# Attention scores from 64-row products of both heads of a pair, without doubled copies of q and k

## The chip, the cores and the metric

The kernel runs on one core of one Trainium2 chip. The core has a tensor engine (PE, with its weight loads listed apart as PEld), a vector engine (DVE), a scalar engine (ACT), GpSimd (POOL) and SyncE (SP, which issues the DMAs). The metric is the time of one execution in microseconds on the device; the kernel before took a median of 1409.52 us in 3 runs (1409.27 to 1410.91).

## The reference, cut to what matters

One layer of a hybrid decoder block on 1024 positions of width 1024, in float32. The attention has 8 heads of 64 and is strictly causal; its weights come from a running sum of log-sigmoids:

```python
def stick_breaking_attention(q, k, v):
    ...
        z = jnp.einsum("bhqd,bhkd->bhqk", qb, kb).astype(jnp.float32) * scale
        ...
        strict = s_idx < t_idx
        log_keep = jnp.where(strict, jax.nn.log_sigmoid(-z), 0.0)
        later = lax.cumsum(log_keep, axis=3, reverse=True) - log_keep
        w = jnp.where(strict, jnp.exp(jax.nn.log_sigmoid(z) + later), 0.0)
        outs.append(jnp.einsum("bhqk,bhkd->bhqd", w, vb.astype(jnp.float32)))

...
        h = rms_norm(x, norm_mix_pre[l])
        proj = h @ w_in[l]
        q, k, v, cb, cc, cx, g_att, g_conv = jnp.split(proj, IN_SPLITS, axis=-1)
        ...
        y_att = o.transpose(0, 2, 1, 3).reshape(b, s, ATT_WIDTH) @ w_att_branch[l]
        y_conv = (cb * causal_dwconv(cc * cx, conv_mix_w[l])) @ w_conv_branch[l]
        merged = jax.nn.sigmoid(g_att) * y_att + jax.nn.sigmoid(g_conv) * y_conv
        x = x + rms_norm(merged @ w_out[l], norm_mix_post[l])
        ...
        u = causal_dwconv(h @ w_up[l], conv_ffn_w[l])
        a, g = jnp.split(u, 2, axis=-1)
        f = (jax.nn.gelu(g, approximate=True) * a) @ w_down[l]
```

## The kernel before, in words

Every float32 matrix product is made from float16 halves: a number is split into a high half (a rounded copy, made by ACT) and a low half (the remainder, made by DVE), and a product takes three passes, high by high, high by low and low by high (`PASSES`). All matmuls use 128 rows of the array, with a weight load (LDWEIGHTS) ahead of each.

The program has these stages: normalising and transposing x, and v of the first four row tiles (to about 50 us); q and k of the first pair of heads (to 75); attention over four pairs `j` of heads (75 to about 420), with other projections mixed in as filling; the two branch products (`pywc`, `pywa`), the gates, the output projection, and then the feed-forward part to the end.

`qk_tile(j, which)` makes q or k of one pair: the 128 rows of its PSUM tile are two heads of 64, in two halves of 512 positions. For q it writes both halves of the split into `qtmp` and then copies each head twice with DVE (L369), so that `XA` and `XB` hold one head each on rows 0 to 63 and again on 64 to 127. For k (L374, L375) each head is a tile `K[:, h]` whose one 64 rows are the high half and the other 64 the low half. One 128-row product of `K` with the doubled high half of q is then both k-high by q-high and k-low by q-high, and a second with the doubled low half adds the other two: two matmuls for a head, four for a pair.

`attention(j)` runs over 12 units in a pair, 48 in all. A unit is one block of 128 keys against up to 512 queries, for both heads (units on the diagonal are 128, 256, 384 or 512 columns wide). `stage1` makes the scores z in PSUM, brings them to SBUF as `zc` (DVE), and takes exp, log and a split of the result, `sp` and `sh` (ACT, ACT, ACT, DVE). `stage2` sums with a triangular matrix into PSUM `A`, adds it to zc (DVE), and makes the split weights `w` (ACT, ACT, DVE); `stage2b` adds the rest of the block to A; `stage3` multiplies by v into PSUM `o`. PSUM holds one z, one A and one o of two banks each, and two banks `pm` for the filling. All these matmuls are recorded at the line of the helper `mm` (L453 before; L439 after the change, since lines move).

`merge` interleaves this with a generator of filling: v of the last four row tiles (in pair 0), q and k of the next pair, and the convolution's projections `pcc`, `pcx` and `pcb`; in pair 3 also `p_split` and the branch products `pywc`. After the last `pcb` matmul the convolution's result `pf` is multiplied (L408), its square summed (`jk_p`, L56), a scale is made through a one-column matmul `pr` (L74 and the small DVE lines behind it), and `p_split` splits it into `p` (L86, L87), which is what `pywc` (L436) reads.

The order on each engine is fixed when the program is built: a scheduler places instructions by priority and by its own estimate of when their inputs are there. Within an engine the order is then strict. `tc.high_priority()` around the attention stages puts them ahead of filling that is ready at the same time. The weights of the projections arrive by DMAs from SP (512 KB each) into a ring of tiles; q, k and most other large tiles come from a ring of 16 slots of 4 KB a row (`slab`).

Of the kernel before, what the change touches and what calls it, by code (L numbers as in the profile page):

```python
# [16 lines left out]
F16 = mybir.dt.float16  # L17
# [3 lines left out]
AF = mybir.ActivationFunctionType  # L21
ALU = mybir.AluOpType
AX = mybir.AxisListType

P = 128
T = 1024
# [8 lines left out]
PASSES = ((0, 0), (0, 1), (1, 0))  # L35


class Layer:
# [230 lines left out]
    def mixer(self, mid):  # L269
        tc, nc, a = self.tc, self.nc, self.a  # L270
        hT = self.hp.tile([P, 2, KD, T], F16, tag="hT", name="hT")
        with ExitStack() as ph1:
# [75 lines left out]
            stk = {}  # L348

            def qk_tile(j, which):  # L350
                w, inv = self.prep(f"{which}{j}")
                if which == "q":
                    stk[j] = dict(A=self.slot([P, 2, T], F16, f"XA{j}"), B=self.slot([P, 2, T], F16, f"XB{j}"),
                                  iq=inv)
                    tmp = self.slot([P, 2, T], F16, f"qtmp{j}")
                else:
                    stk[j]["K"] = self.slot([P, 2, T], F16, f"K{j}")
                s = stk[j]
                for c in range(2):
                    ps = pm.tile([P, NH], F32, tag="pm", name=f"p{which}{j}_{c}")  # L360
                    yield from self.cm_half(w[0], hT, ps, c)
                    sl = ds(c * NH, NH)
                    if which == "q":
                        nc.scalar.activation(tmp[:, 0, sl], ps, AF.Copy, scale=2.0 ** -15)
                        nc.vector.scalar_tensor_tensor(tmp[:, 1, sl], ps, 2.0 ** -15, tmp[:, 0, sl],
                                                       ALU.mult, ALU.subtract)
                        for h0, b in ((0, "A"), (64, "B")):
                            for d0 in (0, 64):
                                nc.vector.tensor_copy(s[b][d0:d0 + 64, :, sl], tmp[h0:h0 + 64, :, sl])  # L369
                    else:  # L370
                        for h0, b in ((0, "A"), (64, "B")):
                            K = s["K"][:, h0 // 64, :]
                            d0 = 64 - h0
                            nc.scalar.activation(K[h0:h0 + 64, sl], ps[h0:h0 + 64], AF.Copy, scale=2.0 ** -15)  # L374
                            nc.vector.scalar_tensor_tensor(K[d0:d0 + 64, sl], ps[h0:h0 + 64], 2.0 ** -15,  # L375
                                                           K[h0:h0 + 64, sl], ALU.mult, ALU.subtract)
                if which == "k":
                    cz = self.small(f"cz{j}", keep=True)
                    self.mul(cz[:, 0:1], s["iq"], inv)
                    self.mul(cz[:, 1:2], cz[:, 0:1], cst[:, 0:1])  # L380
                    s["cz"] = cz[:, 1:2]
                yield
# [61 lines left out]
            def attention(j):  # L444

                s = stk[j]
# [5 lines left out]
                def mm(out, w, mv, **kw):  # L452
                    nc.tensor.matmul(out, w, mv, skip_group_check=True, **kw)  # L453

                def stage1(u):
                    off, i, c, nm = u["off"], u["i"], u["c"], u["nm"]
                    tsl = ds(c * NH + off, NH - off)
                    z = pat.tile([P, 2, NH], F32, tag="z", name=f"z{nm}")
                    for h, b in enumerate("AB"):
                        mm(z[:, h, off:], s["K"][:, h, ds(i * P, P)], s[b][:, 0, tsl], start=True, stop=False)  # L460
                        mm(z[:, h, off:], s["K"][:, h, ds(i * P, P)], s[b][:, 1, tsl], start=False, stop=True)
                    zc = att.tile([P, 2, NH], F32, tag="zc", name=f"zc{nm}", bufs=3)

                    if u["diag"]:
                        nc.vector.scalar_tensor_tensor(zc[:, :, off:], z[:, :, off:], s["cz"],  # L465
                                                       self.clamp[:, :, :NH - off], ALU.mult, ALU.min)
                    else:
                        nc.vector.tensor_scalar(zc[:, :, off:], z[:, :, off:], s["cz"], 44.0,
                                                ALU.mult, ALU.min)

                    sp = att.tile([P, 2, NH], F32, tag="sp", name=f"sp{nm}", bufs=2)
                    nc.scalar.activation(sp[:, :, off:], zc[:, :, off:], AF.Exp)  # L472
                    nc.scalar.activation(sp[:, :, off:], sp[:, :, off:], AF.Ln, bias=self.one)
                    sh = att.tile([P, 2, 2, NH], F16, tag="sh", name=f"sh{nm}", bufs=2)
                    nc.scalar.activation(sh[:, 0, :, off:], sp[:, :, off:], AF.Copy)  # L475
                    nc.vector.tensor_tensor(sh[:, 1, :, off:], sp[:, :, off:], sh[:, 0, :, off:], ALU.subtract)  # L476
                    u["zc"], u["sh"] = zc, sh
# [47 lines left out]
                n = len(units)  # L525
                for k in range(n + 2):
                    if k < n:
                        with tc.high_priority():
                            stage1(units[k])
                        yield 6  # L530
                    if 0 <= k - 1 < n:
                        with tc.high_priority():
                            stage2(units[k - 1])
                        yield 8
                        with tc.high_priority():
                            stage2b(units[k - 1])
                    if 0 <= k - 2 < n:
                        with tc.high_priority():
                            stage3(units[k - 2])
                        yield 6  # L540
# [16 lines left out]
            for which in "qk":  # L557
                for _ in qk_tile(0, which):
                    pass
            for j in range(4):  # L560
                gens = []
                nf = 3 * 16 + 1
                if j == 0:
                    gens += [v_tile(tt) for tt in range(4, 8)]
                    nf += 32
                if j < 3:
                    gens += [qk_tile(j + 1, "q"), qk_tile(j + 1, "k")]
                    nf += 34
                gens.append(conv_tile(j))
                if j == 3:  # L570
                    gens += [p_split()] + [branch(0, d, pm) for d in range(8)]
                    nf += 65
                merge(attention(j), 240, chain(*gens), nf)
# [403 lines left out]
class Pair:  # L977
# [3 lines left out]
    A = {1: (0, 0), 2: (0, 1), 3: (3, 0), 4: (1, 1), 5: (2, 0), 6: (2, 1), 7: (1, 0)}  # L981
# [153 lines left out]
```

## Time and profile before

| what | value |
|---|---|
| median of 3 runs | 1409.52 us (1409.27 to 1410.91) |
| profiled execution, its time | 1407.68 us |
| its span, first to last instruction | 1405.9 us |
| PE busy | 1344.2 us (96%), 6447 matmuls |
| DVE busy | 1083.9 us (77%) |
| ACT busy | 856.6 us (61%) |
| DMA | 99.72 MB, 71 GB/s on average |
| granted PE clock, mean | 0.990 |

An engine is busy while one of its instructions runs; matmuls overlap each other by design, so a busy PE says that matmuls follow each other, and the time from one start to the next says at what rate. Idle time is put down to what released the engine. A row of a group reads: line, engine, operation, output<-inputs, shape, count, busy time in all, mean ns of one, idle time just before them and who ended it.

### The profile page before, as it was taken

To read this page: it belongs to the slowest core of one execution; us is meant where nothing else is said; L and a number is where in the kernel's file an instruction comes from. 1 tells how busy PE (TensorE), PEld (TensorE's weight loads), DVE (VectorE), ACT (ScalarE), POOL (GpSimd) and SP (SyncE) were. 2 spreads that over 40 slices of the span, in tenths; PEclk is the share of its full clock that TensorE was granted. 3 is DMA by queue.
4 is the path that set the end of the run, shared out by engine and by line. 5 is a ranking of instruction groups with operands and counts; after the bars stand their busy time and mean duration, and the time that the engine had idled before them with its cause. 6 is when DMAs were issued, how large, how long until landed. Compare 5 with 4: busy or idle time off the path is not lost. (4 is left out here: it accounts for less than half of the span.)

```text
span 1405.9 us, 16721 instructions
## 1 busy us (share of the span) xinstructions
PE 1344.2 (96%) x6447; PEld 626.9 (45%) x6447; DVE 1083.9 (77%) x1692; ACT 856.6 (61%) x1187; POOL 29.3 (2%) x47
## 2 busy tenths in 40 slices
PE   5999999999989999999998999999999999999997
PEld 3444454545434444444443444444444444444443
DVE  5758787887784797878777894994895796699747
ACT  6568788787873465776556467761761672476422
POOL 2000000000000000000111000000000000000001
PEclk9999999999999999999999999999999999999999
DMA  7111001010001102251331112121220311213115
GB/s 256 46 46 31 31 31 45 31 31 30 31 31 45 31 31 61 90 180 45 106 120 60 60 60 91 60 90 48 89 78 27 121 60 60 108 54 110 60 60 195
DMA packets 28369, 99.72 MB, mean 71 GB/s; under 512 B 3185, under 2 KB 3185, under 8 KB 28289
## 3 DMA queue, kind: packets, MB, share of 16 engines
q1 hardware_dynamic: 27792, 97.01, 20.4%
q0 software_dynamic: 496, 1.65, 0.4%
q8 instruction: 50, 0.82, 0.2%
q14 instruction: 31, 0.25, 0.1%
HBM read 90.25 MB, written 8.39 MB: 70 GB/s over the span
## 5 line engine op out<-in xcount | busy, mean ns | idle before, releaser
L1005 PEld LDWEIGHTS <-wh_u 128*128 128x128 f16 x1848 | 179.2, 98 | 222.7 <-issue 10.2
L904 PE MATMUL pd<-wdh,f 128*128 128x512 f16 x1056 | 234.1, 383 | 9.3 <-DVE wdh L87 5.1
L904 PEld LDWEIGHTS <-f 128*128 128x128 f16 x1056 | 104.1, 99 | 137.5 <-issue 13.3
L86 ACT ACTIVATE wh_u<-ws_u,sc 128x1024 f16<-128x1024 f32 (+1 forms) x66 | 64.2, 999 | 100.7 <-DVE sc L78 83.3
L910 DVE SCALAR_TENSOR_TENSOR yacc<-pd,sd,yacc 128x512 f32<-128x512 f32 x80 | 58.4, 746 | 69.6 <-PE pd L904 62.1
L1005 PEld LDWEIGHTS <-wh_g 128*128 128x128 f16 x588 | 56.8, 98 | 70.6 <-ACT wh_g L86 2.3
L719 PE MATMUL py<-wh_wo,m 128*128 128x512 f16 x384 | 84.7, 381 | 0.0
L87 DVE SCALAR_TENSOR_TENSOR wh_u<-ws_u,sc,wh_u 128x1024 f16<-128x1024 f32 (+1 forms) x66 | 71.8, 1099 | 7.1 <-ACT wh_u L86 7.1
L453 PE MATMUL A<-sh,tri 128*128 128x512 f16 (+3 forms) x352 | 71.5, 323 | 2.9 <-DVE zc L488 1.6
L493 DVE SCALAR_TENSOR_TENSOR w<-zc,w 128x1024 f16<-128x1024 f32 (+3 forms) x48 | 45.8, 955 | 25.0 <-ACT w L492 24.8
L1082 DVE SCALAR_TENSOR_TENSOR ugu<-cgu,cw_g,ugu 128x1023 f32<-128x1023 f32 (+1 forms) x44 | 56.2, 1278 | 10.9 <-ACT ugu L1080 10.5
L472 ACT ACTIVATE sp<-zc 128x1024 f32<-128x1024 f32 (+3 forms) x48 | 40.1, 836 | 29.9 <-DVE zc L465 20.4
L719 PEld LDWEIGHTS <-m 128*128 128x128 f16 x384 | 37.8, 99 | 44.7 <-issue 1.0
L1082 DVE SCALAR_TENSOR_TENSOR ua<-cau,cw_a,ua 128x1023 f32<-128x1023 f32 (+1 forms) x44 | 56.1, 1276 | 1.1 <-ACT ua L1080 1.0
L488 DVE SCALAR_TENSOR_TENSOR zc<-A,zc 128x1024 f32<-128x1024 f32 (+3 forms) x48 | 45.6, 950 | 8.3 <-PE A L453 8.1
L453 PE MATMUL o<-w,v 128*128 128x512 f16 (+3 forms) x192 | 46.0, 329 | 4.4 <-DVE w L493 3.1
L476 DVE TENSOR_TENSOR sh<-sp,sh 128x1024 f16<-128x1024 f32 (+3 forms) x48 | 45.6, 951 | 4.1 <-ACT sh L475 3.8
L309 PE MATMUL pv<-wh_v,hT 128*128 128x512 f16 x192 | 45.7, 389 | 2.5 <-ACT wh_v L86 1.7
L1080 ACT ACTIVATE ua<-cau,cw_a 128x1024 f32<-128x1024 f32 x22 | 25.1, 1139 | 37.1 <-DVE cau L1032 33.8
L56 ACT ACTIVATE jk_u<-ws_u 128x1024 bf16<-128x1024 f32 x44 | 46.3, 1053 | 0.8
L203 PE MATMUL pcx<-hT,wh_cx 128*128 128x512 f16 x192 | 46.3, 379 | 0.2 <-ACT u L404 0.2
L453 PEld LDWEIGHTS <-tri 128*128 128x128 f16 x352 | 32.4, 98 | 30.4 <-issue 3.7
(613 smaller groups left out, 2729.0 us busy)
## 6 DMA issues: line engine op xcount, KB each, us to landing
ws_u<-w_up_nt SPq DMA_DIRECT2D x44, 512.0 KB, 3.5
ds<-w_down SPq DMA_DIRECT2D x22, 512.0 KB, 6.0
wd<-w_down SPq DMA_DIRECT2D x22, 512.0 KB, 3.6
ws_g<-w_in_nt SPq DMA_DIRECT2D x14, 512.0 KB, 3.5
x<-x SPq DMA_DIRECT2D x8, 512.0 KB, 8.8
ws_wo<-w_out SPq DMA_DIRECT2D x8, 512.0 KB, 7.2
xr<-x SPq DMA_DIRECT2D x8, 512.0 KB, 4.1
x2d<-x SPq DMA_DIRECT2D x8, 512.0 KB, 2.9
```

Source lines behind the costliest of these rows:

```text
L56: self.nc.scalar.activation(self.junk(f"jk_{name}"), src, AF.Square, accum_out=acc)
L86: self.nc.scalar.activation(dst[:, 0, :], src, AF.Copy, scale=s)
L87: self.nc.vector.scalar_tensor_tensor(dst[:, 1, :], src, s, dst[:, 0, :], ALU.mult, ALU.subtract)
L203: nc.tensor.matmul(ps, w[:, wi, ds(k * P, P)], hT[:, hi, k, ds(c * NH, NH)], start=n == 0, stop=n == last)
L309: nc.tensor.matmul(pv, hT[:, hi, k, ds(tt * P, P)], wv[k // 2][:, wi, ds((k % 2) * NH, NH)], start=n == 0, stop=n == 3 * KD - 1)
L453: nc.tensor.matmul(out, w, mv, skip_group_check=True, **kw)
L493: nc.vector.scalar_tensor_tensor(w[:, 1, :, off:], zc[:, :, off:], 2.0 ** 14, w[:, 0, :, off:], ALU.mult, ALU.subtract)
L719: nc.tensor.matmul(ps[nh], m16[k][:, hi, ds(tt * P, P)], wo[k][:, wi, ds(nh * NH, NH)], start=k == 0 and p == 0, stop=k == 7 and p == 2)
L904: nc.tensor.matmul(ps, f16[g][k][:, hi, ds(tt * P, P)], w[k][:, wi, sl], start=n == 0, stop=n == 3 * GROUPS[g] - 1)
L910: nc.vector.scalar_tensor_tensor(y[:, sl], ps, sm[:, 0:1], y[:, sl], ALU.mult, ALU.add)
L1005: nc.tensor.matmul(ps, w[wt][:, wi, ds(wc * NH + k * P, P)], self.block(i, hi, k), start=first and n == 0, stop=n == 3 * KH - 1, skip_grou ...
L1082: nc.vector.scalar_tensor_tensor(u[:, lag:], c[:, :T - lag], sm[:, 2 - lag:3 - lag], u[:, lag:], ALU.mult, ALU.add)
```

## The change

q and k of a pair are now kept as they leave the projection: one tile each with the high and the low half, rows 0 to 63 for one head and 64 to 127 for the other. `qtmp`, `XA`, `XB` and the two-headed `K` are gone, and with them the copies; q and k are each converted by one ACT and one DVE instruction of 128 rows for each half of the positions.

The scores of a unit are made in three passes, as everywhere else in the kernel; the low by low product that the doubled tiles gave is left out. In each pass one matmul takes rows 0 to 63 of the array for the first head and one takes rows 64 to 127 for the second, each with its own bank of z. A unit has six matmuls of 64 rows where it had four of 128. A very high priority around each of them puts them ahead of everything else that is ready.

```diff
--- before.py
+++ after.py
@@ -350,30 +350,16 @@
             def qk_tile(j, which):
                 w, inv = self.prep(f"{which}{j}")
                 if which == "q":
-                    stk[j] = dict(A=self.slot([P, 2, T], F16, f"XA{j}"), B=self.slot([P, 2, T], F16, f"XB{j}"),
-                                  iq=inv)
-                    tmp = self.slot([P, 2, T], F16, f"qtmp{j}")
-                else:
-                    stk[j]["K"] = self.slot([P, 2, T], F16, f"K{j}")
+                    stk[j] = dict(iq=inv)
+                stk[j][which] = self.slot([P, 2, T], F16, f"{which}{j}")
                 s = stk[j]
                 for c in range(2):
                     ps = pm.tile([P, NH], F32, tag="pm", name=f"p{which}{j}_{c}")
                     yield from self.cm_half(w[0], hT, ps, c)
                     sl = ds(c * NH, NH)
-                    if which == "q":
-                        nc.scalar.activation(tmp[:, 0, sl], ps, AF.Copy, scale=2.0 ** -15)
-                        nc.vector.scalar_tensor_tensor(tmp[:, 1, sl], ps, 2.0 ** -15, tmp[:, 0, sl],
-                                                       ALU.mult, ALU.subtract)
-                        for h0, b in ((0, "A"), (64, "B")):
-                            for d0 in (0, 64):
-                                nc.vector.tensor_copy(s[b][d0:d0 + 64, :, sl], tmp[h0:h0 + 64, :, sl])
-                    else:
-                        for h0, b in ((0, "A"), (64, "B")):
-                            K = s["K"][:, h0 // 64, :]
-                            d0 = 64 - h0
-                            nc.scalar.activation(K[h0:h0 + 64, sl], ps[h0:h0 + 64], AF.Copy, scale=2.0 ** -15)
-                            nc.vector.scalar_tensor_tensor(K[d0:d0 + 64, sl], ps[h0:h0 + 64], 2.0 ** -15,
-                                                           K[h0:h0 + 64, sl], ALU.mult, ALU.subtract)
+                    nc.scalar.activation(s[which][:, 0, sl], ps, AF.Copy, scale=2.0 ** -15)
+                    nc.vector.scalar_tensor_tensor(s[which][:, 1, sl], ps, 2.0 ** -15, s[which][:, 0, sl],
+                                                   ALU.mult, ALU.subtract)
                 if which == "k":
                     cz = self.small(f"cz{j}", keep=True)
                     self.mul(cz[:, 0:1], s["iq"], inv)
@@ -456,9 +442,12 @@
                     off, i, c, nm = u["off"], u["i"], u["c"], u["nm"]
                     tsl = ds(c * NH + off, NH - off)
                     z = pat.tile([P, 2, NH], F32, tag="z", name=f"z{nm}")
-                    for h, b in enumerate("AB"):
-                        mm(z[:, h, off:], s["K"][:, h, ds(i * P, P)], s[b][:, 0, tsl], start=True, stop=False)
-                        mm(z[:, h, off:], s["K"][:, h, ds(i * P, P)], s[b][:, 1, tsl], start=False, stop=True)
+                    for n, (hk, hq) in enumerate(PASSES):
+                        for h in range(2):
+                            d = ds(64 * h, 64)
+                            with tc.high_priority(10 ** 6):
+                                mm(z[:, h, off:], s["k"][d, hk, ds(i * P, P)], s["q"][d, hq, tsl],
+                                   start=n == 0, stop=n == 2)
                     zc = att.tile([P, 2, NH], F32, tag="zc", name=f"zc{nm}", bufs=3)
 
                     if u["diag"]:
```

Three places in the order show the effect. Names end in a buffer number; `z0_01` is the unit of pair 0 with key block 1, `A`, `sh`, `tri`, `o` and `v16` belong to attention's later stages, `pv`, `pcb` and `pywc` are filling. On PE, the scores of unit z0_01 before:

```order
L309 MATMUL pv5_738<-wh_v_3_182,hT_101 128x512
L453 LDWEIGHTS K0_611
L453 MATMUL z0_01_746<-XA0_497,K0_611 128x384
...
L453 LDWEIGHTS tri_98
L453 MATMUL A0_03_716<-sh0_03_684,tri_98 128x128
...
L453 MATMUL z0_01_746<-XB0_498,K0_611 128x384
```

The same unit in the changed program:

```order
L309 MATMUL pv5_728<-wh_v_2_179,hT_101 128x512
L439 LDWEIGHTS k0_601
L439 MATMUL z0_01_736<-q0_497,k0_601 128x384
...
L309 LDWEIGHTS hT_101
L309 MATMUL pv5_728<-wh_v_2_179,hT_101 128x512
```

The load and the matmul of z stand there six times in a row, with nothing between; before, matmuls of A stood among the four. That holds for all 48 units: before, 12 of them had other work inside, now none has.

On PE at the end of attention (pair 3, last key block 0), before:

```order
L436 MATMUL pywc0_1_3485<-p16_3_3432,wh_wc0_0_2891 128x512
L453 LDWEIGHTS v16_0_113
L453 MATMUL o3_17_3479<-w3_10_3885,v16_0_113 128x512
L436 LDWEIGHTS wh_wc0_0_2891
L436 MATMUL pywc0_0_3462<-p16_3_3432,wh_wc0_0_2891 128x512
```

And in the changed program:

```order
L203 MATMUL pcb3_1_3386<-hT_101,wh_cb3_0_2772 128x512
L439 LDWEIGHTS v16_0_113
L439 MATMUL o3_17_3509<-w3_10_3925,v16_0_113 128x512
...
L74 LDWEIGHTS ones_85
L74 MATMUL pr26_3448<-rb26_3445,ones_85 128x1
L74 LDWEIGHTS ones_85
L74 MATMUL pr27_3477<-rb27_3475,ones_85 128x1
L422 LDWEIGHTS wh_wc0_0_2905
L422 MATMUL pywc0_0_3492<-p16_0_3453,wh_wc0_0_2905 128x512
```

The last `o` matmuls of attention stood among the first `pywc`; now they stand right behind the last `pcb`, and between them and the first `pywc` there are only the two one-column matmuls `pr`.

On ACT at the same place, before:

```order
L492 ACTIVATE w3_12_3759<-zc3_12_3653 128x1024
L56 ACTIVATE jk_p3_3412,sm_p_449<-pf3_3301 128x1024
L56 ACTIVATE jk_wa2_0_3458,sm_wa2_3455<-ws_wa2_0_3456 128x1024
L472 ACTIVATE sp3_10_3805<-zc3_10_3803 128x1024
L473 ACTIVATE sp3_10_3805<-sp3_10_3805,one_89 128x1024
L490 ACTIVATE zc3_11_3734<-zc3_11_3734 128x1024
L475 ACTIVATE sh3_10_3808<-sp3_10_3805 128x1024
L492 ACTIVATE w3_11_3823<-zc3_11_3734 128x1024
L86 ACTIVATE p16_0_3423<-pf0_1440,sc25_3414 128x1024
```

In the changed program:

```order
L481 ACTIVATE w3_10_3925<-zc3_10_3843 128x1024
L507 ACTIVATE of3_10_3964<-o3_17_3509 64x512
L56 ACTIVATE jk_p3_3442,sm_p_449<-pf3_3327 128x1024
L507 ACTIVATE of3_10_3964<-o3_17_3509 64x512
L56 ACTIVATE jk_wa2_0_3488,sm_wa2_3485<-ws_wa2_0_3486 128x1024
L511 ACTIVATE o16_3_3036<-of3_10_3964 128x512
L86 ACTIVATE p16_0_3453<-pf0_1436,sc25_3444 128x1024
```

The square of pf (`jk_p3`) stood ahead of the last unit of attention on ACT and now stands behind it.

## The prediction

> **What bounds the kernel now.** I read the whole page first, then the busy time by stage, then what the tensor engine waits for inside the attention stage, then the order in time of its matmuls. The page first:
>
> ```profile
> span 1405.9 us, 16721 instructions
> PE 1344.2 (96%) x6447; PEld 626.9 (45%) x6447; DVE 1083.9 (77%) x1692; ACT 856.6 (61%) x1187; POOL 29.3 (2%) x47
> ```
>
> PE is busy nearly all the time, but a share over the span does not say whether it is the limit where the change is made. The scores are made between 75 and 400 us. The table by stage gives busy time with the number of instructions in brackets; the last three columns are granted PE clock, DMA share and GB/s:
>
> ```profile
> 75.00:400.00 325.00, 320.42 (x1685) 157.94 (x1683) 259.22 (x385) 261.35 (x351) 0.00 (x0) 1.00 0.10 31
> 400.00:420.00 20.00, 15.52 (x63) 6.35 (x62) 18.23 (x32) 16.55 (x20) 0.00 (x0) 0.91 0.08 27
> 420.00:480.00 60.00, 56.64 (x265) 25.53 (x264) 30.00 (x56) 23.20 (x38) 0.00 (x0) 1.00 0.15 45
> ```
>
> In the first row PE lacks 4.6 us of 325, while DVE and ACT are idle for 66 and 64. So in this stage a microsecond of PE work added or taken moves everything behind it, and a microsecond of DVE or ACT work does so only where PE waits for it. The second row is the end of attention, the one place where PE is short of work. All that PE waits for in the first row:
>
> ```profile
> PE A L453 <- DVE zc L488: 1.2, 2, 0.9
> PE z L453 <- DVE K L375: 0.9, 1, 0.9
> PE o L453 <- DVE w L493: 0.9, 1, 0.9
> PE o L453 <- ACT w L492: 0.7, 1, 0.7
> PE z L453 <- DVE zc L465: 0.6, 2, 0.4
> ```
>
> Eight short waits. Only one, 0.9 us for K, comes from the operands that the change makes differently.
>
> How much PE time a matmul takes is read from runs of equal matmuls in order of time (start, length, count):
>
> ```profile
> 149.52 0.28 PE L453 MATMUL z<-XA,K 128*128 128x128 f16 x2
> 150.18 1.89 PE L453 MATMUL A<-sh,tri 128*128 128x512 f16 x8
> 151.91 1.46 PE L203 MATMUL pcc<-hT,wh_cc 128*128 128x512 f16 x6
> 154.09 0.38 PE L453 MATMUL z<-XA,K 128*128 128x256 f16 x2
> 291.76 0.81 PE L453 MATMUL A<-sh,tri 128*128 128x384 f16 x4
> ```
>
> Eight of 512 columns begin at 150.18 and the next group at 151.91: 0.216 us from start to start. One record is 0.379 long (the group lasts 1.89 = 7 x 0.216 + 0.38). So a matmul needs 0.216 of the array and its result is there 0.379 after its start; the missing 0.163 lies beside the next matmul. The other widths give (0.81 - 0.326) / 3 = 0.162 for 384 columns, 0.38 - 0.272 = 0.109 for 256 and 0.28 - 0.219 = 0.06 for 128 (I use 0.056), with record lengths from 219 ns up:
>
> ```profile
> L453 PE MATMUL z<-XA,K x96: 219/351/379, 74.9 to 399.8; 128*128 128x512 f16 x48, 128*128 128x128 f16 x16, 128*128 128x256 f16 x16, 128*128 128x384 f16 x16
> L453 PE MATMUL z<-XB,K x96: 219/352/379, 76.0 to 400.2; 128*128 128x512 f16 x48, 128*128 128x128 f16 x16, 128*128 128x256 f16 x16, 128*128 128x384 f16 x16
> ```
>
> **The change part by part.** *Score matmuls.* Now 192 are issued: 96 x 0.216 + 32 x (0.162 + 0.109 + 0.056) = 31.2 us, four to a unit. The change issues six to a unit, 288. If the two of a pass share the array, a unit costs three spacings instead of four: 23.4 us, so -7.8. If they follow each other it costs six: 46.8, so +15.6. No row shows a 64-row product. The nearest is the weight load:
>
> ```profile
> L453 PEld LDWEIGHTS <-tri 128*128 128x128 f16 x352 | 32.4, 98 | 30.4 <-issue 3.7
> ```
>
> 98 ns of load for every matmul disappear inside the 0.216 spacing, so the array does take a second instruction while one streams, and the two of a pass touch different rows and different PSUM banks. I take -7.8. The Trainium skill (TensorE: Matmul & The Clock Gate, section Measured speedup vs the span model) reports row-packed matmuls as running side by side; no trace here shows it yet.
>
> *Going between 128 and 64 rows.* Each of the 48 units now goes into the 64-row shape and out of it: 96 turns, where before every matmul had one shape. The new order keeps the six together, so there are no more than 96. A turn costs nothing if the pipeline takes it like any other weight load, and at least the hidden 0.163 if the array must run empty first: 0 to 15.6 us, and with an exposed 98 ns load behind it 25.1. Nearest row: the trace has no other change of shape to go by, and the longest pipeline time that it does show is the 0.163; I take that, +15.6, and keep 0 and 25.1 for the range. The Trainium skill (TensorEngine Tiling (Array Packing), section Key Properties) says that a change of tiling mode drains the TensorE, without a price; by that rule the full 0.163 falls due and the sum stays as it is, without it the sum would be about -8.
>
> *Copies of q and k.* Mean ns stand before the last bar's idle time:
>
> ```profile
> L375 DVE SCALAR_TENSOR_TENSOR K<-pk,K 64x512 f16<-64x512 f32 x16 | 11.0, 689 | 4.0 <-ACT K L374 3.6
> L374 ACT ACTIVATE K<-pk 64x512 f16<-64x512 f32 x16 | 9.4, 590 | 1.3 <-PE pk L203 0.7 <-DVE K L375 0.4
> L369 DVE COPY XB<-qtmp 64x1024 f16<-64x1024 f16 x16 | 6.8, 423 | 0.2
> L369 DVE COPY XA<-qtmp 64x1024 f16<-64x1024 f16 x16 | 6.7, 417 | 0.2
> ```
>
> Gone are 32 copies (13.5 us) and 8 of the 16 K remainders (5.5) on DVE, and 8 activations (4.7) on ACT; one on 128 rows replaces two on 64, and I keep the duration. This lies beside PE work in the first stage, so nearly all of it is worth nothing. What it does give is the K wait at the first scores, -0.9. No DMA, POOL or SP instruction comes or goes.
>
> *The end of attention.* Freed DVE time lets the scheduler run attention further ahead of the projections that fill PE. Before, the last scores stood after the last projection pcb, and the last `A` and `o` mixed with waits: in the second stage row 61 full matmuls x 0.216 = 13.2 of 20 us, so 6.8 lost (part of it to the clock of 0.91). In the new order 48 pcb matmuls cover those steps, and these 6.8 go. But the last pcb also begins another chain: pf, its sum of squares, the scale, the split of p, and only then pywc. It used to run while attention finished. Now three `o` matmuls stand behind the last pcb, then PE stops. Durations of that chain, from before:
>
> ```profile
> 399.16 0.75 DVE L408 SCALAR_TENSOR_TENSOR pf<-pcb,cv,pf 128x512 f32<-128x512 f32 x1 [1.15 <-PE pcb L203]
> 401.07 1.04 ACT L56 ACTIVATE jk_p<-pf 128x1024 bf16<-128x1024 f32 x1
> 402.02 0.19 ACT L56 ACTIVATION_READ_ACCUMULATOR jk_p<-pf 128x1 f32 x1
> 402.24 1.06 ACT L56 ACTIVATE jk_wa<-ws_wa 128x1024 bf16<-128x1024 f32 x1
> 403.72 0.15 DVE L68 TENSOR_REDUCE sc<-sm_p 128x1 f32<-128x4 f32 x1
> 404.92 0.14 DVE L69 CAST rb<-sc 128x1 bf16<-128x1 f32 x1
> 405.91 0.19 PE L74 MATMUL pr<-rb,ones 128*128 128x1 bf16 x2
> 408.26 4.25 ACT L86 ACTIVATE p<-pf,sc 128x1024 f16<-128x1024 f32 x4
> 409.71 1.28 DVE L87 SCALAR_TENSOR_TENSOR p<-pf,sc,p 128x1024 f16<-128x1024 f32 x1
> 418.94 0.59 ACT L518 ACTIVATE of<-o 64x512 f32<-64x512 f32 x1 [3.36 <-PE o L453]
> 421.94 0.63 ACT L522 ACTIVATE o<-of 128x512 f16<-128x512 f32 x1 [0.76 <-DVE of L519]
> ```
>
> By ACT's new order, counted from the end of the last pcb (t = 0): the `o` matmuls free PE at 0.5 and end at 0.65; ACT does of until 1.3, then the square of pf and its read until 2.5; reduce and cast on DVE, so pr starts at 2.8: PE waited 2.3. ACT goes on with of (3.1), jk_wa (4.3), o16 (4.9) and p (6.0): pywc starts near 6.0, another 2.9. Its third pass needs the remainder on DVE, 1.28 later, about 1 more, and the next tile's somewhat less. Together 6.6. With nothing queued ahead on ACT the least is 3.6, and with a half-clock stretch as at 400 us 8.5. Taken 7.5, against 6.8 before: +0.7 (-3.2 to +1.7).
>
> *Sum.* -7.8 + 15.6 - 0.9 + 0.7 = +7.6 us on the profiled execution, which took 1407.7 us (1.8 around its span of 1405.9). It lies 1.8 below the 1409.5 median of the runs; I add the difference to that median: 1417.1, said as 1417. The remaining waits of the first stage are left at 3.7: PE gets slower there, so they could shrink to nothing or, with six scores now in one piece, grow a little.
>
> **The rivals.**
> 1. *The turn is cheap, so the kernel gets faster.* Place: the first 128-row matmul behind each six. For it: no row shows a drain, and dtype changes (the bf16 pr between f16 matmuls) cost none. Against: all pipelining in the trace is between matmuls of one shape. Without the 15.6 the sum is -8.0, 1401.5 us; it is zero at 8.0 / 96 = 83 ns a turn. The gain may not all arrive, since the shorter PE work meets the chain of DVE and ACT earlier; doubling the 3.7 us of waits would give 1405.
> 2. *The two of a pass follow each other.* +15.6 in place of -7.8: 1424.9 if turns are free, 1440.5 with them. For it: line 453's matmuls never overlap beyond 0.163. Against: the disjoint rows and banks.
> 3. *Weight loads no longer hide.* Passes two and three of a unit would each show one or two loads of 98 ns: 48 x 2 x 0.098 = 9.4, or 18.8, so 1426.5 to 1435.9. Against: the 98 ns are hidden everywhere now. The Trainium skill (TensorE: Matmul & The Clock Gate, section The mechanism) lets a load overlap a running matmul only when the row groups differ; this trace, where loads to the same 128 rows hide, already disagrees, which is why I give it little.
> 4. *The relief of DVE decides and PE does not.* Against: the 4.6 us of waits in 325. At most those go as well, 1413 with my turn price; it is inside my range.
>
> **How the numbers follow.** A change under 0.2% (2.8 us) can hardly be told from none. Per turn price: above 112 ns the sum is over +2.8, below 54 ns under -2.8. Chances: forecast, pairs share the array and a turn costs 112 to 260 ns (1412 to 1427), 0.55; the same with 54 to 112 ns, no change, 0.14; rival 1 below 54 ns, 0.13; rival 2, 0.10; rival 3, 0.08. Slower 0.55 + 0.10 + 0.08 = 0.73, same 0.14, faster 0.13. The range 1408 to 1431 leaves out rival 1 and the upper halves of rivals 2 and 3, about 0.2.
>
> **What would show it.** Pairs: the two z records of a pass start within some ns and a unit of 512 columns takes 3 x 0.216. Turns: from the last z to the next matmul, and from the matmul before to the first z, 0.379 or more instead of 0.216. Relief: no copies, and the first scores without the 0.9 wait. End: pr waits some 2.3 and pywc some 2.9 us after attention, near 415 to 425. I am wrong if these turns show 0.216 to 0.27, if six z take 1.3 us, or if waits for DVE grow well beyond 4.6 us between 75 and 400.

## The result, and the profile after

The changed kernel takes 1413.17 us (median of 7 runs, 1410.43 to 1414.92) against 1409.27 for the kernel before on the same chip (7 runs, 1406.69 to 1410.91). The ratio is 1.0031, 95% interval 1.0017 to 1.0044: slower by some 4.4 us by this ratio and by 3.9 by the two medians, where +7.6 was forecast. The profiled execution has a span of 1410.9 us, 5.0 more than before.

The first two lines of the page, after:

```profile
span 1410.9 us, 16871 instructions
PE 1345.0 (95%) x6543; PEld 616.1 (44%) x6543; DVE 1065.5 (76%) x1652; ACT 852.0 (60%) x1179; POOL 29.9 (2%) x47
```

There are 96 matmuls more and 40 DVE instructions less, as the change says; DVE works 18.4 us less, and the time is longer all the same. Where it goes shows in busy time by stage. From 73 to 400, 400 to 430 and 430 to 480 us, first before, then after:

```profile
73.00:400.00 327.00, 322.42 (x1694) 158.85 (x1693) 259.66 (x387) 262.83 (x353) 0.00 (x0) 1.00 0.10 32
400.00:430.00 30.00, 24.68 (x106) 10.54 (x105) 23.72 (x43) 21.56 (x28) 0.00 (x0) 0.94 0.07 21
430.00:480.00 50.00, 47.48 (x223) 21.34 (x221) 24.51 (x44) 18.18 (x29) 0.00 (x0) 1.00 0.17 52
```

```profile
73.00:400.00 327.00, 320.58 (x1771) 147.05 (x1768) 247.40 (x356) 263.61 (x350) 0.00 (x0) 1.00 0.10 30
400.00:430.00 30.00, 23.60 (x98) 9.92 (x97) 18.47 (x38) 12.20 (x17) 0.00 (x0) 0.89 0.11 35
430.00:480.00 50.00, 47.48 (x223) 21.54 (x222) 22.21 (x43) 18.04 (x29) 0.00 (x0) 1.00 0.14 43
```

The third row is alike in both. In the first PE idles 6.4 us instead of 4.6; in the second, where attention ends, it idles 6.4 instead of 5.3 at a clock of 0.89 instead of 0.94.

How the scores stand on the array shows one unit of 512 columns in order of time, on PE and then on its weight loads, in the kernel after:

```profile
109.76 1.03 PE L203 MATMUL pq<-hT,wh_q 128*128 128x512 f16 x4
110.72 0.82 PE L439 MATMUL z<-q,k 64*128 64x512 f16 x6
111.48 0.60 PE L203 MATMUL pq<-hT,wh_q 128*128 128x512 f16 x2
```

```profile
109.98 0.31 PEld L203 LDWEIGHTS <-wh_q 128*128 128x128 f16 x2
110.72 0.33 PEld L439 LDWEIGHTS <-k 64*128 64x128 f16 x6 [0.42 <-DVE zc L477]
111.47 0.33 PEld L203 LDWEIGHTS <-wh_q 128*128 128x128 f16 x3 [0.42 <-issue]
```

Six matmuls last 0.82 us: two spacings of 0.22 and one record of 0.376. The raw starts behind this row are 110.722, 110.726, 110.949, 110.952, 111.165 and 111.168, so the two of a pass begin 3 or 4 ns apart and share the array. On both sides there is a step: the last `pq` began at 110.41 and the first score at 110.72, 0.31 instead of 0.216, and from the last score to the next `pq` it is again 0.31. Every undisturbed turn of this run costs 0.095 to 0.096, counted from the start of a pass, after 128 columns as after 512; after a one-column matmul it is 0.07. The loads tell how: among equal shapes the next load starts 2 ns after the running matmul, but across a turn none starts until 0.307 after the last matmul began, that is 0.09 after its columns have passed and 0.07 before its record ends; the matmul then follows the load by 4 ns. So at a turn nothing new enters for 0.09 us, and the stop of 0.096 is shorter than the 0.163 that waiting for the last result would take; the ends of matmul records are modelled, so how empty the array then is the trace does not show. The Trainium skill (TensorEngine Tiling (Array Packing), section Key Properties) says that a change of tiling mode drains the TensorE. This trace agrees in that the stream stops at every turn; the price here is 96 ns.

Adding up the starts of all matmuls between the first score and the first gate (`pgc`), with 0.216, 0.162, 0.109 and 0.056 for a matmul and for each turn what it measured, 0.07 to 0.096:

| from the first score to the first gate, us | before | after |
|---|---|---|
| score matmuls | 31.2 | 24.0 |
| all other matmuls | 357.0 | 357.4 |
| turns | 0 | 8.8 (95) |
| the rest: waits and half clock | 16.8 | 21.1 |
| sum | 404.9 | 411.3 |

The 0.4 more of other matmuls are two of `pk` that now stand behind the first scores. The first score starts 2.0 us earlier after the change (1.7 of it is a stretch at half clock near 50 us that only the profile of before has), and the later stages differ by 0.6.

The end of attention, on which the prediction's last term rested, after:

```profile
408.37 0.81 PE L439 MATMUL o<-w,v 128*128 128x512 f16 x3
408.57 0.75 DVE L394 SCALAR_TENSOR_TENSOR pf<-pcb,cv,pf 128x512 f32<-128x512 f32 x1 [3.71 <-PE pcb L203]
409.71 1.04 ACT L56 ACTIVATE jk_p<-pf 128x1024 bf16<-128x1024 f32 x1
411.28 0.22 PE L74 MATMUL pr<-rb,ones 128*128 128x1 bf16 x2 [2.11 <-DVE rb L71]
413.06 4.25 ACT L86 ACTIVATE p<-pf,sc 128x1024 f16<-128x1024 f32 x4
414.24 1.01 PE L422 MATMUL pywc<-p,wh_wc 128*128 128x512 f16 x2 [2.74 <-ACT p L86]
415.56 4.81 PE L422 MATMUL pywc<-p,wh_wc 128*128 128x512 f16 x11 [0.31 <-DVE p L87]
```

The three `o` matmuls, 2.1 us of nothing, `pr`, 2.7 us of nothing, then `pywc`, whose first eleven are spaced at half clock (4.81 us).

### The profile page after: what moved, and what is told of

The parts are those of the page before. It is cut to its first block, busy times and chain, and to the rows that moved or that the text cites. A ratio compares the mean times of both kernels' runs of the same rounds, so it can differ in the third digit from the quotient of the medians.

```text
span 1410.9 us, 16871 instructions
## 1 busy us (share of the span) xinstructions
PE 1345.0 (95%) x6543; PEld 616.1 (44%) x6543; DVE 1065.5 (76%) x1652; ACT 852.0 (60%) x1179; POOL 29.9 (2%) x47
## 5 line engine op out<-in xcount | busy, mean ns | idle before, releaser
L482 DVE SCALAR_TENSOR_TENSOR w<-zc,w 128x1024 f16<-128x1024 f32 (+3 forms) x48 | 45.8, 954 | 18.4 <-ACT w L481 18.3
L422 PE MATMUL pywc<-p,wh_wc 128*128 128x512 f16 x192 | 45.1, 395 | 6.0 <-ACT p L86 2.7
L479 ACT ACTIVATE zc<-zc 128x1024 f32<-128x1024 f32 (+3 forms) x48 | 40.0, 834 | 11.5 <-DVE zc L477 11.2
```

The lines of the kernel that those rows point to most:

```text
L482: nc.vector.scalar_tensor_tensor(w[:, 1, :, off:], zc[:, :, off:], 2.0 ** 14, w[:, 0, :, off:], ALU.mult, ALU.subtract)
```

## The experiments

Two theories stood against each other. **A**: PE limits the attention stage, so the 9 us of turns count in full and outweigh what the pairs save. **B**: PE stops being the limit once it has less to do, turns are partly taken up in waits for DVE and ACT, and the order at the end of attention, which the freed DVE brings about, carries much of the loss.

Every ratio is to the kernel before on the chip of that run. A difference between two ratios therefore carries both intervals, 0.16 to 0.19% or about 2.5 us. The differences given below are clear of that unless said otherwise, but their sizes are rough.

**Twice the turns.** A zero column is multiplied and added into z after the first pass, so that a unit leaves the 64-row shape once more (the lines that make the column `zcol` are not shown).

```diff
                     for n, (hk, hq) in enumerate(PASSES):
+                        if n == 1:
+                            with tc.high_priority(10 ** 6):
+                                mm(z[:, 0, off:off + 1], self.tri[:, 0, :], self.zcol, start=False, stop=False)
                         for h in range(2):
```

> After the first pass of each unit a 128-row matmul of one column of zeros is added into z; the result does not change, but the unit has four turns instead of two (192 in all). Theory A: 96 x 0.096 + 48 x 0.03 = +10.6 us over the changed kernel, about 1424 (1.010). Theory B: the added PE time is partly taken up by waits that now end earlier, +2 to +5 us, 1415 to 1418.

Measured: 1416.48 us, ratio to before 1.0052 (1.0039 to 1.0065), 0.21% or 3 us over the changed kernel. In order of time a unit now reads:

```profile
115.40 0.39 PE L441 MATMUL z<-q,k 64*128 64x512 f16 x2
115.72 0.18 PE L441 MATMUL z<-zcol,tri 128*128 128x1 f16 x1
115.83 0.61 PE L441 MATMUL z<-q,k 64*128 64x512 f16 x4
116.37 0.61 PE L441 MATMUL A<-sh,tri 128*128 128x256 f16 x4
```

From the first score to the next `A` it takes 0.97 us instead of 0.76: 0.21 for two more turns and the column, 10.1 for 48 units. Of these only 3 reach the end. The row by stage shows where the rest went: PE idles 0.6 us between 73 and 400 instead of 6.4.

```profile
73.00:400.00 327.00, 326.38 (x1803) 149.68 (x1802) 244.23 (x349) 259.32 (x346) 0.00 (x0) 1.00 0.10 30
```

A is wrong in its "in full": with PE slower the waits for DVE vanish. So these 10 us of added PE time were worth about a third of themselves, with the margin given above; taken as a rule it would not hold for more, since there are only 6.4 us of waits to use up.

**Without the very high priority.**

```diff
-                            with tc.high_priority(10 ** 6):
-                                mm(z[:, h, off:], s["k"][d, hk, ds(i * P, P)], s["q"][d, hq, tsl],
-                                   start=n == 0, stop=n == 2)
+                            mm(z[:, h, off:], s["k"][d, hk, ds(i * P, P)], s["q"][d, hq, tsl],
+                               start=n == 0, stop=n == 2)
```

> The change without the very high priority around the score matmuls: the scheduler then puts other work among the six of a unit, and the program has 156 turns between 64 and 128 rows instead of 96. Theory A (a turn costs 96 ns of a stage that PE limits): 60 more turns are +5.8 us over the changed kernel, about 1419 (1.007 of before). Theory B (PE is not the limit once it has less to do, turns are mostly taken up by waits for DVE and ACT): within 2 us of the changed kernel, 1411 to 1415. Either way the single turn should again show about 96 ns.

Measured: 1417.17 us, ratio 1.0069 (1.0055 to 1.0083), 0.38% or 5.4 us over the changed kernel, which is A's figure. The 60 turns are 5.8 us by the price found above, but the work put between also separates pairs, which A had not counted: score matmuls come to 27.4 us instead of 24.0. Of 9.2 us on PE somewhat more than half reaches the end, so this run fits neither A's "in full" nor B's 2 us. Keeping the six together is worth having.

**Both heads in turn instead of side by side in the order.**

```diff
-                    for n, (hk, hq) in enumerate(PASSES):
-                        for h in range(2):
+                    for h in range(2):
+                        for n, (hk, hq) in enumerate(PASSES):
```

> The changed kernel with the loops over passes and heads exchanged: the three passes of one head, then those of the other, so that neighbours are on the same 64 rows except at the one seam. If only neighbours on different rows share the array: 5 spacings for a unit instead of 3, 39.0 us of score matmuls instead of 23.4 (starts 0.216 apart for 512 columns, one pair a few ns apart), +15 us of PE work less what waits take up: 1418 to 1428. If PE starts the other head's matmuls ahead of their place in the order: the time of the changed kernel.

Measured: 1411.29 us, ratio 1.0024 (1.0014 to 1.0034), not to be told from the changed kernel. The six matmuls of 512 columns still last 0.83 us:

```profile
138.89 1.03 PE L203 MATMUL pcc<-hT,wh_cc 128*128 128x512 f16 x4
139.85 0.83 PE L439 MATMUL z<-q,k 64*128 64x512 f16 x6
140.61 0.82 PE L203 MATMUL pcc<-hT,wh_cc 128*128 128x512 f16 x3
```

They start in pairs 10 ns apart with 0.216 between pairs. Matmuls of 512 columns on the same rows start 0.216 apart wherever these traces show them, so each pair must be one of either head: the second head's first matmul, fourth in the order, starts beside the first head's first. The records name no head, so this is inferred from the pairs. Pairing does not hang on the order within the six. That the order within an engine is strict, as the description of the kernel before has it, is therefore not so for matmuls on different rows of the array.

**The scores in one piece, with 128-row products.** The kernel before with the high priority alone.

```diff
-                        mm(z[:, h, off:], s["K"][:, h, ds(i * P, P)], s[b][:, 0, tsl], start=True, stop=False)
-                        mm(z[:, h, off:], s["K"][:, h, ds(i * P, P)], s[b][:, 1, tsl], start=False, stop=True)
+                        for n in range(2):
+                            with tc.high_priority(10 ** 6):
+                                mm(z[:, h, off:], s["K"][:, h, ds(i * P, P)], s[b][:, n, tsl],
+                                   start=n == 0, stop=n == 1)
```

> The kernel before with the very high priority around its four score matmuls, so that the scores of a unit stand in one piece as in the change, with 128-row products and the copies. If the placing alone costs time: 2 to 4 us over before. If it is the 64-row shape and the freed DVE: within 1.5 us of before.

Measured: 1406.29 us, ratio 0.9985 (0.9976 to 0.9994). That is 0.15% or some 2 us faster, more than the 1.5 expected at most. The placing costs nothing, so it is not the cause of the loss; it saves a little. Measured against this run, the 64-row products with the freed DVE cost 0.46% instead of 0.31%.

**The copies put back.** DVE gets the 32 copies of q back, into tiles that nobody reads; the scores stay as changed. The two tiles that take the copies (their lines are not shown) also hold two more slots of the ring for each pair.

```diff
+                    if which == "q":
+                        for h0, b in ((0, "A"), (64, "B")):
+                            for d0 in (0, 64):
+                                nc.vector.tensor_copy(s[b][d0:d0 + 64, :, sl], s["q"][h0:h0 + 64, :, sl])
```

> The changed kernel with the 32 DVE copies of q put back (into tiles that nobody reads) and two more slab tiles for each pair, so DVE has 13.5 us more to do and the scores are still made by six 64-row matmuls. If the copies cost nothing beside PE: the time of the changed kernel, 1412 to 1414. If what the relief of DVE did to the order at the end of attention (the p chain with nothing to cover it) is a part of the loss: 2 to 4 us faster than the changed kernel, 1409 to 1411, although more work is done. If DVE is the limit after all: slower than 1415.

Measured: 1409.8 us, ratio 1.0008 (1.0000 to 1.0017): more work, and 0.23% or 3.2 us faster than the changed kernel. With DVE loaded nearly as before the scheduler leaves attention almost as far behind its filling as it was, and the first `pywc` run again right behind the last `A` and among the last `o`:

```profile
409.43 0.81 PE L444 MATMUL A<-sh,tri 128*128 128x512 f16 x3 [0.98 <-DVE sh L470]
411.10 0.59 PE L427 MATMUL pywc<-p,wh_wc 128*128 128x512 f16 x2 [0.86 <-ACT p L86]
412.74 5.73 PE L427 MATMUL pywc<-p,wh_wc 128*128 128x512 f16 x18 [1.05 <-DVE p L87]
418.31 0.38 PE L444 MATMUL o<-w,v 128*128 128x512 f16 x1
```

That the lighter DVE led to a worse order, and not only that it did not help, is what this run adds. No timed run separates the copies from the two slots; built with the slots alone, the program keeps the changed kernel's order at the end of attention. The whole loss of the change is about the size of this gain.

**The p chain shortened.** The scale of p comes from the first three of its four tiles (with one power of two of room), so three tiles are split before the last projection. The same edit was made to the kernel before.

```diff
-                s_, inv = self.scale_of(smp_, 4, keep=True)
...
+                if 0 in js:
+                    psc["s"], inv_x[0] = self.scale_of(smp_, 3, keep=True, slack=1)
+                    acts[0] = []
+                for j in js:
...
+                if j == 3:
+                    gens.append(p_split(range(3)))
                 gens.append(conv_tile(j))
                 if j == 3:
+                    gens += [p_split((3,))] + [branch(0, d, pm) for d in range(8)]
```

> The changed kernel with the scale of p taken from the first three of the four tiles' square sums (with one power of two of headroom), so that p of tiles 0 to 2 is split before the last projection and only the fourth tile's split stands behind the last pcb matmul. If the end of attention carries a part of the loss: pr no longer waits 2.3 and pywc no longer 2.9 us, 3 to 6 us faster than the changed kernel, 1407 to 1410. If turns carry it all: at most 1 us faster.

Measured on the changed kernel: 1408.07 us, ratio to before 0.9999 (0.9989 to 1.0009), 0.32% or 4.5 us under the changed kernel. Of the two waits, 2.1 and 2.7 us, one of 0.84 is left, and the clock stays at 1.00 through 400 to 430 us:

```profile
410.45 0.81 PE L442 MATMUL o<-w,v 128*128 128x512 f16 x3
411.10 0.59 PE L203 MATMUL pcb<-hT,wh_cb 128*128 128x512 f16 x2
411.54 0.17 PE L74 MATMUL pr<-rb,ones 128*128 128x1 bf16 x1
412.54 5.34 PE L425 MATMUL pywc<-p,wh_wc 128*128 128x512 f16 x24 [0.84 <-DVE pf L394]
```

> The kernel before with the early scale of p (three of four square sums), no 64-row products. The p chain is already covered by attention's end there, so if the chain matters only where nothing covers it: within 2 us of before. If the split of four tiles of p on ACT and DVE also holds up the last attention units (it stands between them on both engines): 4 to 6 us faster, 1403 to 1405, and then it beats both kernels.

Measured on the kernel before: 1403.64 us, ratio 0.9963 (0.9949 to 0.9977), 5 us faster; the second reading holds. So this edit is worth much the same with and without the change, and with it on both sides the change still costs 0.36% (0.9999 against 0.9963). The p chain is therefore not what only the changed kernel pays: before, it held up the last units of attention instead of standing bare behind them. What remains of the loss then is turns against pairs, and above all waits: from the first score to the first gate it is 405.8 us against 400.0 with the early scale on both sides, at full clock in both. Added up as in the table, turns less pairs give 1.6 of the difference, the two `pk` 0.4 and waits 3.8. Why the waits grow though DVE has less to do was not separated further.

**The relief without the turns.** As the run before, with the copies of q for pairs 1 to 3 made by DMAs from the POOL queue.

```diff
-                                nc.vector.tensor_copy(s[b][d0:d0 + 64, :, sl], tmp[h0:h0 + 64, :, sl])
+                                if j == 0:
+                                    nc.vector.tensor_copy(s[b][d0:d0 + 64, :, sl], tmp[h0:h0 + 64, :, sl])
+                                else:
+                                    nc.gpsimd.dma_start(s[b][d0:d0 + 64, :, sl], tmp[h0:h0 + 64, :, sl])
```

> As the run before, and with the copies of q for pairs 1 to 3 made by DMAs from the POOL queue instead of DVE: the DVE relief of the change (10 of its 13.5 us of copies) without a single turn between 64 and 128 rows. If the relief is worth something where PE has no turns to pay: 1 to 2 us faster than the run before, 1402 to 1404. If relief only moves attention ahead of its filling: the same or slower.

Measured: 1398.17 us, ratio 0.9931 (0.9919 to 0.9943), 10.5 us faster than the kernel before and 0.32% faster than with the early scale alone, more than the 1 to 2 us expected. It beats both kernels. PE idles 4.0 us between 73 and 400 instead of 5.9, and 1.8 instead of 0.9 from 400 to 430. The rows are first of the kernel with DMA copies, then of the one with the early scale alone:

```profile
73.00:400.00 327.00, 323.00 (x1698) 159.19 (x1697) 255.91 (x383) 268.23 (x361) 14.06 (x24) 1.00 0.15 41
400.00:430.00 30.00, 28.19 (x132) 12.75 (x131) 20.08 (x31) 18.20 (x24) 0.00 (x0) 1.00 0.12 36
```

```profile
73.00:400.00 327.00, 321.11 (x1687) 158.06 (x1686) 262.78 (x405) 265.22 (x357) 0.00 (x0) 1.00 0.10 32
400.00:430.00 30.00, 29.13 (x137) 13.14 (x136) 20.77 (x27) 18.64 (x23) 0.00 (x0) 1.00 0.12 36
```

These two profiled spans are only 1.0 us apart (1396.5 and 1397.5), less than the medians, so how much of the 5 us the stage itself gives stays open. Shown is that moving the copies off DVE makes the kernel faster where no turns are paid and the p chain is short; that this is DVE time and not another order of the program is argued.

## Why the prediction was right, and where it was off

*Pairs, -7.8.* Right: measured -7.2. The two of a pass start 3 to 4 ns apart; rival 2 is out. The missing 0.6 is the first spacing of a unit (0.226 instead of 0.216) and one unit that waited in its middle.

*Turns, +15.6.* The step "I take that" of 0.163 was mis-sized: a turn measured 0.096, 96 of them 9.2 us. The stop is shorter than the 0.163, and the row nearest to the case was the wrong ruler. That alone takes 6.4 from the sum. The order kept its 96 turns as said. Rival 1 would have needed 83 ns or less by its own sum; the measured turn is just beyond. A start of 0.312 also lies between the sign that was named for the forecast (0.379 or more) and the one against it (0.216 to 0.27), and 96 ns falls into the branch of 54 to 112 ns that was given 0.14 and no change, not into the one of 112 to 260 that was forecast.

*Loads (rival 3).* Out: the loads of passes two and three start with the matmuls of the pass before and stay hidden.

*Relief, -0.9, and rival 4.* The K wait is gone from the list of what PE waits for. After:

```profile
PE A L439 <- DVE zc L477: 1.8, 4, 0.8
PE o L439 <- DVE w L482: 1.7, 2, 0.9
PE pk L203 <- DVE q L361: 1.3, 1, 1.3
PE z L439 <- DVE zc L457: 1.2, 2, 0.6
PE z L439 <- DVE zc L454: 0.3, 1, 0.3
```

But "in this stage a microsecond of PE work moves everything behind it" was too strong, and with it the remaining waits "left at 3.7": they are 6.3, which gives back 2.6 of what went. Half of that is one wait of 1.3 for the split of q (L361), which the list before does not have: what went with K came back at q. The list before has 4.6, so growing to 6.3 it also puts rival 4 out, by which the waits should have gone; that its 1413 is the measured time is chance. Doubling the turns cost 10.1 us on PE and 3 at the end. Putting the copies back made the kernel faster, so the relief, through the order, cost time.

*The end of attention, +0.7.* The mechanism is as predicted to a few tenths: starts of `pr` 2.3 and of `pywc` 2.9 us late, by the waits and starts shown. Of the 7.5 that was taken, 6.6 had been added up from rows; the 0.9 above that lay between this and the case with a half-clock stretch and has no row of its own. Sized by the rows of 400 to 430 us the term is nearer +2.6: idle 6.4 instead of 5.3, and at 0.89 instead of 0.94 of the clock 3.3 us instead of 1.8 lost to it. The half-clock stretch there lasts 6.8 us after the change and 3.4 before.

*Sum.* -7.2 + 9.2 + 2.6 + 2.6 - 0.9 = +6.3, which is the +6.4 of the table (there the turns are 8.8, since one lies outside and seven behind one-column matmuls are shorter, and the two `pk` are 0.4); less 2.0 at the start and with 0.6 later it is the 5.0 of the spans. The direction and the place were right; the sum was too high because the turn was priced too high, and two smaller terms were too low. That the direction held is in part luck: with a turn of 96 ns and all else as it stood, the prediction's own sum is +1.2, which it calls no change. The waits and the end of attention, missed by 2.6 and 1.9, made up for most of the 6.4 that the turn was too dear.

What stays open: what the change would give if a turn cost nothing, which no run here shows, and why PE waits longer in the attention stage while DVE has less to do.

## What to carry to other kernels

Two 64-row products do run side by side, but entering and leaving that shape costs about 0.1 us each time, so a group of them must save more than 0.2 us: three passes of 512 columns for two heads against four 128-row ones save 0.216 of PE time and just break even, narrower ones lose. Work taken from an engine that is not the limit is not free of effect where a scheduler orders by estimated readiness: look at what the freed time lets run ahead, and which chain then stands bare at the stage's end. Before reshaping products, move copies to an idle DMA queue and shorten the chain at the seam; here that gave 0.7% where the reshaping cost 0.3%.

## What the runs showed of the hardware that was not expected

A turn between 128- and 64-row matmuls costs 0.095 to 0.096 us in the changed kernel whatever the width before it, 0.07 after a one-column matmul (up to 0.107 in the run without the very high priority); the next weight load is held until 0.307 us after the start of a 512-column matmul instead of 2 ns.

Matmuls on different 64 rows do not keep to the program's order among each other: with one head's three matmuls placed ahead of the other's, they still started in pairs 10 ns apart.

Weight loads for the two halves of the rows also start together, 3 ns apart, each recorded at 92 to 96 ns.
